# A list scheduler inside a two-block transformer kernel is run ten times, with backward priorities and margins in its cost table

## The chip, the cores and the metric

The kernel runs on one core of a Trainium2 chip. The metric is the device time of one execution in microseconds (us), less is better. Five engines run their own instruction streams and meet at semaphores: TensorE (PE in the rows, its weight loads PEld), VectorE (DVE), ScalarE (ACT), GpSimd (POOL) and SyncE (SP, which only issues transfers).

## What is computed

A sequence of 512 tokens of width 1024 passes two layers of a first block and one layer of a second block, all in fp32, and a final RMS norm. Cut to what matters:

```python
for l in range(2):                                   # first block
    sh1, sc1, gt1, sh2, sc2, gt2 = split(silu(c) @ w_ada[l] + b_ada[l])
    h = rms_norm(x) * (1 + sc1) + sh1
    dn_qkv, dn_z, dn_a, dn_b, sw_q, sw_k, sw_v, gate_a, gate_b = split(h @ w_in[l])
    o_dn = gated_delta_rule(l2(conv(dn_qkv)), g, beta)       # 8 heads of 128, state S
    y_a = (rms_norm(o_dn) * silu(dn_z)) @ w_dn_out[l]
    y_b = swa_sink_attention(sw_q, sw_k, sw_v) @ w_swa_out[l]   # window 128
    x = x + gt1 * ((sig(gate_a) * y_a + sig(gate_b) * y_b) @ w_o[l])
    h = rms_norm(x) * (1 + sc2) + sh2
    a, b = split(h @ w_up[l])                                # 2 x 2816
    x = x + gt2 * ((silu(conv(a)) * b) @ w_down[l])
# second block: band attention + S5 state space + GLU, gated merge, w_out, rms_norm
```

The delta rule is a recurrence over chunks: the state after one chunk is needed for the next (`v_new = u - w S; o = q S + qk v_new; S = S exp(g) + k^T v_new`), and inside a chunk a triangular system is solved.

## The kernel before, in words

**Matmuls.** Each fp32 operand is split in a high and a low part. A weight piece arrives by DMA as `raw` (128x1024), ACT rounds it to `whi`, and DVE takes `wlo = raw - whi`; activations give `hhi` and `hlo` in the same way. A product is then three matmuls, `hhi*whi`, `hlo*whi`, `hhi*wlo`, each with 512 columns, summed in PSUM in a tile `gf` (or `gt`, where the weights stand still). These are the bulk of TensorE's work, and they need nothing of the serial steps around them.

**The delta rule.** Two heads and four chunks at a time (a head pair) go through one chain, b = 0 to 3. On TensorE it reads: `yps` and `zps` in 32x32 tiles, twice, then `wps`, then `yps` and `zps` in 64x64 tiles (the inverse of the triangular system), then for each of four chunks `xps`, `osps`, `osps`, `kqs` (the recurrence). Each step's result is taken from PSUM by ACT (`y`, `yy`, `xs`, `qd`) or DVE (`xf`, `wf`, `st`, `pp`) before the next step can start. The products `qk` and the like of a chain are kept in four buffers of the tag `qk`; the evicted gate products `mb` use the buffers of that same tag.

**Attention and norms.** `sc` are scores, `pp` probabilities, `ptr` their transposes, `pc` and `pv` DVE's copies of them, `pvo` the product with the values. At the borders of the stages (mixing to FFN, FFN to mixing, FFN to the second block) the residual `x` is normed: `nsum` (the factor), `xn` (DVE), its transposes `ntr` (TensorE), again `xn` with scale and shift, then `hhi` (ACT) and `hlo` (DVE). Every weight product of the next stage needs these.

**The order.** Nothing of the order is written by hand. The program is recorded first: class `Recorder` keeps each engine call as an `Op` with its dependencies, the tiles it uses, and a duration from a table (`cost`). `plan` (line 202) is a greedy list schedule: at each step it takes the engine whose next ready op can start first, and on it the op of the least `prio`, which is the op's number in the program plus a bias that the network gives. A tile's buffers are given out in the order in which the program first uses the tiles of a tag. `emit` then issues all ops in the planned order (line 359, the line of every instruction in the profile) and fixes on each engine the order and who follows whom in each buffer. At run time each engine takes its instructions strictly in that order. So an instruction whose operand is late holds all that stands behind it on its engine.

## Time and profile before

| what | us |
|---|---|
| median of 3 runs | 2430.78 |
| lowest and highest | 2430.03, 2432.83 |
| profiled execution | 2433.17 |
| its span | 2431.4 |

The span reaches from the first to the last instruction of the profiled execution; 1.8 us lie around it. In the rows further down, a PE that is not busy is waiting, and the name behind the arrow is what released it. Matmuls overlap by their pipeline, so that the step from start to start, not the duration, is what one costs in a row of them. `f32` is named for both fp32 and the rounded form. In the rows of windows the granted clock (1.00 is TensorE's full 2.4 GHz, 0.50 the lower level of 1.2 GHz) is the third number from the end, behind the busy times of PE, PEld, DVE, ACT and POOL with their counts.

### The profile page before, as it was taken

To read this page: it belongs to the slowest core of one execution; us is meant where nothing else is said; L and a number is where in the kernel's file an instruction comes from. 1 tells how busy PE (TensorE), PEld (TensorE's weight loads), DVE (VectorE), ACT (ScalarE), POOL (GpSimd) and SP (SyncE) were. 2 spreads that over 40 slices of the span, in tenths; PEclk is the share of its full clock that TensorE was granted. 3 is DMA by queue.
4 is the path that set the end of the run, shared out by engine and by line. 5 is a ranking of instruction groups with operands and counts; after the bars stand their busy time and mean duration, and the time that the engine had idled before them with its cause. 6 is when DMAs were issued, how large, how long until landed. Compare 5 with 4: busy or idle time off the path is not lost.

```text
span 2431.4 us, 35819 instructions
## 1 busy us (share of the span) xinstructions
PE 2364.1 (97%) x13388; PEld 1928.4 (79%) x13388; DVE 1644.6 (68%) x3087; ACT 1012.2 (42%) x2095; POOL 522.9 (22%) x719
## 2 busy tenths in 40 slices
PE   7999999999999999999999999999999998999998
PEld 4878777778888887887888787888888888877786
DVE  3898899676666577468888955566555546765454
ACT  5544454533443233354446454334323323264432
POOL 1322424204100000213232421050051613500000
PEclk9999999999999999999999999999999999999999
DMA  7322225456446556332222333445334344532242
GB/s 251 99 66 77 84 71 161 139 168 200 156 153 197 180 181 187 118 103 74 66 75 79 89 111 96 130 170 184 114 109 127 117 146 146 173 113 79 78 139 78
DMA packets 239742, 309.10 MB, mean 127 GB/s; under 512 B 32144, under 2 KB 189712, under 8 KB 239568
## 3 DMA queue, kind: packets, MB, share of 16 engines
q1 hardware_dynamic: 228864, 275.64, 37.0%
q0 software_dynamic: 10416, 30.91, 3.5%
q8 instruction: 106, 1.74, 0.3%
q14 instruction: 68, 0.56, 0.1%
q10 hardware_dynamic: 288, 0.26, 0.0%
HBM read 276.20 MB, written 30.56 MB: 126 GB/s over the span
## 4 chain that ended last, share of the span: by engine, by line
PE 84%; DVE 7%; DMA 3%; ACT 2%; issue 2%; SPq 1%; POOL 1%; DVEq 0%; POOLq 0%; ACTq 0%
PE gf L359 54%; PE gt L359 18%; PE sc L359 1%; SPq L359 1%; PE pvo L359 1%; PE ada L359 1%; DMA pn<-nd 1%; PE zps L359 1%; PE osps L359 1%; PE kqs L359 1%; PE yps L359 1%; DVE wlo L359 1%; PE qktr L359 1%; PE gram L359 1%; DVE ua L359 1%
## 5 line engine op out<-in xcount | busy, mean ns | idle before, releaser
L359 PE MATMUL gf<-hhi,whi 128*128 128x512 f32 (+1 forms) x1888 | 720.8, 384 | 11.8 <-ACT whi L359 8.5
L359 PE MATMUL gf<-hlo,whi 128*128 128x512 f32 (+1 forms) x1888 | 720.6, 382 | 0.2 <-DVE hlo L359 0.2
L359 PE MATMUL gf<-hhi,wlo 128*128 128x512 f32 (+1 forms) x1888 | 719.9, 382 | 0.1
L359 DVE TENSOR_TENSOR wlo<-raw,whi 128x1024 fp32r<-128x1024 f32 (+1 forms) x358 | 461.8, 1291 | 339.2 <-ACT whi L359 336.1
L359 ACT ACTIVATE whi<-raw 128x1024 fp32r<-128x1024 f32 (+1 forms) x366 | 378.6, 1036 | 655.7 <-PE gf L359 310.5
L359 PEld LDWEIGHTS gf<-hhi,whi 128*128 128x128 f32 x1888 | 358.3, 191 | 76.2 <-ACT whi L359 10.0
L359 PEld LDWEIGHTS gf<-hlo,whi 128*128 128x128 f32 x1888 | 359.1, 190 | 60.7 <-issue 2.1
L359 PEld LDWEIGHTS gf<-hhi,wlo 128*128 128x128 f32 x1888 | 359.0, 190 | 59.4 <-DVE wlo L359 0.6
L359 PE MATMUL gt<-whi,g 128*128 128x512 f32 x704 | 220.1, 392 | 0.0
L359 PEld LDWEIGHTS gt<-whi,g 128*128 128x128 f32 x704 | 132.2, 188 | 27.2
L359 PE MATMUL gt<-wlo,g 128*128 128x512 f32 x352 | 137.4, 390 | 0.0
L359 DVE SCALAR_TENSOR_TENSOR acc<-raw,csil,acc 128x1024 f32<-128x1024 f32 x70 | 90.7, 1295 | 34.8 <-DMA raw<-in_w_ada_dram 34.6
L359 DVE SCALAR_TENSOR_TENSOR cacc<-gf,vec,cacc 128x511 f32<-128x511 f32 x144 | 106.8, 743 | 7.9 <-ACT cacc L359 6.6
L359 PE MATMUL gt<-whi,hhi 128*128 128x512 f32 (+1 forms) x288 | 107.1, 374 | 1.0 <-DVE gx L359 1.0
L359 PE MATMUL gt<-wlo,hhi 128*128 128x512 f32 (+1 forms) x288 | 107.6, 374 | 0.0
L359 PE MATMUL gt<-whi,hlo 128*128 128x512 f32 (+1 forms) x288 | 107.5, 375 | 0.0
L359 PE MATMUL gf<-rhi,whi 128*128 128x512 f32 x256 | 99.9, 390 | 0.0
L359 PE MATMUL gf<-rhi,wlo 128*128 128x512 f32 x256 | 99.8, 390 | 0.0
L359 PE MATMUL gf<-rlo,whi 128*128 128x512 f32 x256 | 99.8, 390 | 0.0
L359 DVE SCALAR_TENSOR_TENSOR facc<-gf,vec,facc 128x511 f32<-128x511 f32 x88 | 65.7, 748 | 37.2 <-ACT facc L359 35.6
L359 PEld LDWEIGHTS gt<-wlo,g 128*128 128x128 f32 x352 | 66.2, 188 | 13.5 <-issue 0.2
L359 POOL DMA_DIRECT2D acc<-in_b_ada_dram x4 | 2.1, 525 | 288.3 <-DVE wlo L359 283.5
(414 smaller groups left out, 3802.4 us busy)
## 6 DMA issues: line engine op xcount, KB each, us to landing
raw<-in_w_in_dram SPq DMA_DIRECT2D x140, 512.0 KB, 3.7
raw<-in_w_ada_dram SPq DMA_DIRECT2D x80, 512.0 KB, 4.0
raw<-in_w_up_dram SPq DMA_DIRECT2D x80, 512.0 KB, 4.2
raw<-in_w_down_dram SPq DMA_DIRECT2D x40, 512.0 KB, 3.7
wa<-in_w_ada_dram SPq DMA_DIRECT2D x32, 256.0 KB, 6.0
raw<-in_w_dn_out_dram SPq DMA_DIRECT2D x16, 512.0 KB, 3.5
raw<-in_w_swa_out_dram SPq DMA_DIRECT2D x16, 512.0 KB, 4.8
raw<-in_w_o_dram SPq DMA_DIRECT2D x16, 512.0 KB, 3.8
```

What stands on the lines that cost most here:

```text
L359: i = f(*a, **k).ins
```

## The change

The kernel's network, its instructions and its `cost` table stay. Only the planner is rewritten:

- `plan` is split. `prepare` builds what every schedule shares; `schedule(tags)` is the greedy pass, with buffers handed out in the order of `tags`; `late(seq)` walks a finished schedule backwards and gives each op the latest start that would not move its end, from the next op on its engine, its dependents, and the tile that follows in each of its buffers.
- `plan` now makes ten schedules. After each, the buffer order becomes the order of first use in that schedule, and the priority of each op becomes half its old priority (for the first, its start) plus half its latest start. The schedule with the least planned end goes out; here it is the third of the ten.
- `MARGIN`: 30 ns are added to each planned duration on every engine but TensorE. `SLACK`: 30 ns more on each crossing from one engine to another; it was zero.

```diff
-SLACK = {"PE": 0.0, "DVE": 0.0, "ACT": 0.0, "POOL": 0.0, "SP": 0.0}
+MARGIN, SLACK = 30.0, 30.0
+ROUNDS = 10
...
+    def schedule(self, tags):
...
+        place = {nm: (g, k) for g, names in tags.items() for k, nm in enumerate(names)}
...
-                since[tag, k] = t = heapq.heappop(freed[tag])
+                since[tag, k], old = heapq.heappop(freed[tag])
+                self.then[old] = tags[tag][k]
...
-                d = o.dur
+                d = o.dur + (0 if e == PE_E else MARGIN)
...
-                    q.ready = max(q.ready, clock[e] if q.eng == e == PE_E else end + LAT[q.eng] + (0 if q.eng == e else SLACK[q.eng]))
+                    q.ready = max(q.ready, clock[e] if q.eng == e == PE_E else end + LAT[q.eng] + (0 if q.eng == e else SLACK))
...
+    def late(self, seq):
+
+        late, after = {}, {}
+        for o in reversed(seq):
+            took, x = o.end - o.start, self.end
+            f = after.get(o.eng)
+            if f is not None:
+                x = late[f.n] - min(f.start - o.start, o.dur - o.over)
+            for q in o.succ:
+                if q.eng != o.eng or q.eng != PE_E:
+                    x = min(x, late[q.n] - took - LAT[q.eng])
+            for t in o.tiles:
+                if t.name in self.then:
+                    x = min(x, late[self.first[self.then[t.name]]] - took - 60)
+            late[o.n] = x
+            after[o.eng] = o
+        return late
+
+    def plan(self):
+
+        self.prepare()
+        tags, best = self.tags, None
+        for k in range(ROUNDS):
+            seq = self.schedule(tags)
+            if seq is None:
+                break
+            if best is None or self.end < best[0]:
+                best = self.end, seq
+            self.first, tags = {}, {}
+            for o in seq:
+                for t in o.tiles:
+                    if t.name not in self.first:
+                        self.first[t.name] = o.n
+                        tags.setdefault(t.tag, []).append(t.name)
+            late = self.late(seq)
+            for o in self.ops:
+                o.prio = 0.5 * ((o.prio if k else o.start) + late[o.n])
+        self.end, seq = best
         return seq
```

What this does to the streams is seen in the orders. Both programs hold the same matmuls; the FFN stages stand nearly as they stood, and most of what moved lies in the mixing stages of the first block and in the second block. The number of places where TensorE goes from one tile size to another falls from 213 to 186.

**First place: TensorE, last head pair (b = 3) of layer 0.** Before, the recurrence stands among the weight products `gf`. From the first chunk's `xps` (rows at TensorE's number 1344 and following):

```order
1344 L359 MATMUL xps<-vk,wf 128x128 x2
1345 L359 MATMUL gf<-hhi,wlo 128x512
1346 L359 MATMUL gf<-hhi,whi 128x512
1347 L359 MATMUL gf<-hlo,whi 128x512
1348 L359 MATMUL osps<-xs,kd 128x128 x2
1349 L359 MATMUL osps<-xs,ua 128x128 x2
1350 L359 MATMUL gf<-hhi,wlo 128x512
1351 L359 MATMUL gf<-hhi,whi 128x512
1352 L359 MATMUL gf<-hlo,whi 128x512
1353 L359 MATMUL gf<-hhi,wlo 128x512
1354 L359 MATMUL kqs<-st,qk 128x128 x4
```

Now the whole chain of this head pair stands bare, together with the last attention product in front of it; ahead of these rows stand four `ada` and eight `ptr`, and behind them three more rounds of `xps`, `osps`, `osps`, `kqs` follow before the next `gf` (number 1438):

```order
1417 L406 MATMUL pvo<-pc,swv 64x512 x2
1418 L406 MATMUL pvo<-pv,swv 64x512 x2
1419 L406 MATMUL yps<-xf,um 32x32 x32
1420 L406 MATMUL zps<-y_941,wf 32x32 x32
1421 L406 MATMUL yps<-xf,um 32x32 x16
1422 L406 MATMUL zps<-yy,wf 32x32 x16
1423 L406 MATMUL wps<-cst,xf 128x128 x8
1424 L406 MATMUL yps<-xf,ua 64x64 x8
1425 L406 MATMUL zps<-wf,yy 64x64 x8
1426 L406 MATMUL xps<-vk,wf 128x128 x2
1427 L406 MATMUL osps<-xs,kd 128x128 x2
1428 L406 MATMUL osps<-xs,ua 128x128 x2
```

What moved: the `gf` that stood between the steps have gone ahead of the chain or behind it. From the transposes to the last `kqs` no weight product is left to run while a step's result is being taken from PSUM.

**Second place: TensorE, the last rounds of the last head pair of layer 1.** Before, a few `gf` stand between every two steps:

```order
5192 L359 MATMUL xps<-pp,wf 128x128 x2
5193 L359 MATMUL gf<-hhi,whi 128x512
5194 L359 MATMUL gf<-hlo,whi 128x512
5195 L359 MATMUL gf<-hhi,wlo 128x512
5196 L359 MATMUL osps<-xs,kd 128x128 x2
5197 L359 MATMUL osps<-xs,ua 128x128 x2
5198 L359 MATMUL gf<-hhi,whi 128x512
5199 L359 MATMUL gf<-hlo,whi 128x512
5200 L359 MATMUL gf<-hhi,wlo 128x512
5201 L359 MATMUL kqs<-st,qk 128x128 x4
5202 L359 MATMUL gf<-hhi,whi 128x512
```

Now two rounds have none between them:

```order
5282 L406 MATMUL xps<-pp,wf 128x128 x2
5283 L406 MATMUL gf<-hlo,whi 128x512
5284 L406 MATMUL gf<-hhi,wlo 128x512
5285 L406 MATMUL osps<-xs,kd 128x128 x2
5286 L406 MATMUL osps<-xs,ua 128x128 x2
5287 L406 MATMUL kqs<-st,qk 128x128 x4
5288 L406 MATMUL xps<-pp,wf 128x128 x2
5289 L406 MATMUL osps<-xs,kd 128x128 x2
5290 L406 MATMUL osps<-xs,ua 128x128 x2
5291 L406 MATMUL kqs<-st,qk 128x128 x4
5292 L406 MATMUL gf<-hhi,whi 128x512
```

What moved: seven steps in a row stand without a `gf`.

**Third place: VectorE, the border from mixing to FFN in layer 0.** Here `xn` of the last tokens is what TensorE's `ntr` wait for. Before, two low parts `wlo` and both `hlo` stand between `nsum` and that `xn`:

```order
974 L359 TENSOR_TENSOR x<-x,xm 128x512
975 L359 TENSOR_SCALAR xn<-ntr,modc 128x128 x4
976 L359 TENSOR_TENSOR nsum<-nss 128x1
977 L359 TENSOR_TENSOR wlo<-raw,whi 128x1024 x2
978 L359 TENSOR_TENSOR hlo<-xn,hhi 128x4x128 x2
979 L359 TENSOR_SCALAR xn<-x,nsum 128x512 x2
980 L359 TENSOR_TENSOR wlo<-raw,whi 128x1024
981 L359 TENSOR_SCALAR xn<-ntr,modc 128x128 x4
```

Now:

```order
976 L406 TENSOR_TENSOR x<-x,xm 128x512
977 L406 TENSOR_SCALAR xn<-ntr,modc 128x128 x4
978 L406 TENSOR_SCALAR xn<-x,nsum 128x512
979 L406 TENSOR_TENSOR nsum<-nss 128x1
980 L406 TENSOR_TENSOR wlo<-raw,whi 128x1024
981 L406 TENSOR_TENSOR hlo<-xn,hhi 128x4x128
982 L406 TENSOR_SCALAR xn<-x,nsum 128x512 x2
983 L406 TENSOR_TENSOR hlo<-xn,hhi 128x4x128
984 L406 TENSOR_SCALAR xn<-ntr,modc 128x128 x4
```

What moved: one of the two `wlo` and one of the two `hlo` now stand behind that `xn`. On TensorE five rows of `gf` with 256 columns now stand ahead of the first `ntr` there, where `ntr` was the first.

## Rows read from the trace of the kernel before

**Rows 1.** page, engines: busy us (share of the span), instructions

```profile
...
PE 2364.1 (97%) x13388; PEld 1928.4 (79%) x13388; DVE 1644.6 (68%) x3087; ACT 1012.2 (42%) x2095; POOL 522.9 (22%) x719
...
```

**Rows 2.** stages: length, busy PE PEld DVE ACT POOL; granted clock, DMA share, GB/s

```profile
...
0.00:61.00 61.00, 46.95 (x241) 29.05 (x242) 19.60 (x44) 36.30 (x64) 12.09 (x18) 1.00 0.80 251
61.00:525.00 464.00, 453.29 (x3136) 362.51 (x3135) 395.63 (x955) 226.09 (x623) 136.44 (x139) 1.00 0.35 103
525.00:1060.00 535.00, 522.35 (x2499) 437.94 (x2498) 341.64 (x446) 187.39 (x271) 57.53 (x104) 0.98 0.54 170
1060.00:1504.00 444.00, 439.24 (x3102) 352.64 (x3101) 359.40 (x893) 219.48 (x610) 126.36 (x123) 1.00 0.30 85
1504.00:2060.00 556.00, 545.69 (x2655) 458.95 (x2654) 304.04 (x394) 193.29 (x279) 144.72 (x294) 0.98 0.42 137
2060.00:2420.00 360.00, 354.75 (x1759) 286.13 (x1758) 220.57 (x352) 148.93 (x250) 45.07 (x41) 1.00 0.35 112
...
```

**Rows 3.** what PE waited for: total us, times, longest

```profile
...
PE ntr L359 <- DVE xn L359: 11.2, 7, 4.0
...
PE gf L359 <- ACT whi L359: 8.5, 4, 3.2
...
```

**Rows 4.** same columns as Rows 2, around the dips of the clock

```profile
...
440.00:450.00 10.00, 7.76 (x27) 5.16 (x26) 9.32 (x28) 3.55 (x4) 0.52 (x1) 0.83 0.58 173
648.00:660.00 12.00, 7.61 (x42) 7.11 (x41) 10.53 (x20) 7.51 (x16) 2.04 (x2) 0.72 0.77 257
1028.00:1045.00 17.00, 10.90 (x57) 9.14 (x56) 14.05 (x29) 12.41 (x27) 3.91 (x4) 0.80 0.47 142
1644.00:1656.00 12.00, 8.41 (x52) 8.12 (x53) 9.69 (x19) 6.10 (x14) 2.04 (x2) 0.72 0.77 262
2019.00:2034.00 15.00, 9.79 (x46) 9.08 (x47) 11.07 (x24) 7.16 (x17) 4.48 (x3) 0.67 0.44 140
...
```

**Rows 5.** DVE and PE, first border between mixing and FFN: start, duration, idle before

```profile
650.63 2.35 DVE L359 TENSOR_TENSOR wlo<-raw,whi 128x1024 fp32r<-128x1024 f32 x2
...
654.64 1.75 PE L359 MATMUL ntr<-cst,xn 128*128 128x128 f32 x7 [1.16 <-DVE xn L359]
...
```

**Rows 6.** PE and DVE, last delta chain of layer 0: start, duration, operation

```profile
390.13 0.76 PE L359 MATMUL yps<-xf,um 128*32 128x32 f32 x64
...
402.86 3.00 DVE L359 TENSOR_TENSOR wlo<-raw,whi 128x1024 fp32r<-128x1024 f32 x1 [0.36 <-ACT whi L359]
...
403.51 1.14 PE L359 MATMUL zps<-wf,yy 64*64 64x64 f32 x16
...
407.21 0.60 PE L359 MATMUL xps<-vk,wf 128*128 128x128 f32 x4
...
411.80 0.68 PE L359 MATMUL xps<-pp,wf 128*128 128x128 f32 x4
...
417.30 0.39 PE L359 MATMUL xps<-pp,wf 128*128 128x128 f32 x2
...
420.83 1.13 PE L359 MATMUL kqs<-st,qk 128*128 128x128 f32 x8
...
```

**Rows 7.** that stretch in the columns of Rows 2, then gf alone

```profile
...
390.00:422.00 32.00, 32.00 (x370) 25.64 (x369) 29.53 (x69) 16.44 (x34) 14.07 (x24) 1.00 0.60 179
...
390.00:422.00 32.00, 21.99 (x76) 13.27 (x77) 1.27 (x2) 2.28 (x4) 1.00 0.60 179
...
```

**Rows 8.** PE, attention of layer 0, before and between two tiles

```profile
...
519.05 1.27 PE L359 MATMUL ptr<-cst,pp 128*128 128x128 f32 x8
...
522.77 1.08 PE L359 MATMUL pvo<-pc,swv 128*64 128x512 f32 x4
...
```

**Rows 9.** PE, around one piece of 128x32 tiles

```profile
...
394.42 0.39 PE L359 MATMUL gf<-hhi,whi 128*128 128x512 f32 x1
394.65 0.40 PE L359 MATMUL gf<-hlo,whi 128*128 128x512 f32 x1
394.98 0.70 PE L359 MATMUL yps<-xf,um 128*32 128x32 f32 x32
...
```

More of the change, by code (lines that the diff above doesn't have):

```diff
@@ L57 @@
 class Op:
-    __slots__ = ("n", "eng", "name", "call", "dur", "over", "lock", "dep", "succ", "left", "ready", "tiles", "need", "prio", "start", "mode", "bytes", "team", "lead", "wait", "tables")
+    __slots__ = ("n", "eng", "name", "call", "dur", "over", "lock", "dep", "succ", "left", "ready", "tiles", "need", "prio", "start", "end", "mode", "bytes", "team", "lead", "wait", "tables")
 class Eng:
@@ L199, in add, with prepare @@
         return o
-    def plan(self):
-        import heapq
+    def prepare(self):
         ops = self.ops
         for o in ops:
-            o.left = len(o.dep)
-            o.ready = 0.0
             for p in o.dep.values():
                 p.succ.append(o)
-        uses, order, bufs, place = {}, {}, {}, {}
+        self.uses, self.bufs, self.tags = {}, {}, {}
         for o in ops:
-            o.need = []
             for t in o.tiles:
                 nm = t.name
-                if nm not in uses:
-                    uses[nm] = 0
-                    tag = t.tag
-                    order.setdefault(tag, []).append(nm)
-                    bufs[tag] = t.bufs or t.tag_meta.bufs
-                    place[nm] = tag, len(order[tag]) - 1
-                uses[nm] += 1
-                o.need.append(place[nm])
+                if nm not in self.uses:
+                    self.uses[nm] = 0
+                    self.tags.setdefault(t.tag, []).append(nm)
+                    self.bufs[t.tag] = t.bufs or t.tag_meta.bufs
+                self.uses[nm] += 1
         pend = None
@@ L235, in plan @@
                 pend = (o, key) if o.mode != (128, 128) else None
+    def schedule(self, tags):
+        import heapq
+        ops, bufs = self.ops, self.bufs
+        uses = dict(self.uses)
+        place = {nm: (g, k) for g, names in tags.items() for k, nm in enumerate(names)}
         for o in ops:
-            o.left -= sum(p.lead is o.lead for p in o.dep.values())
+            o.need = [place[t.name] for t in o.tiles]
+            o.ready = 0.0
+            o.left = len(o.dep) - sum(p.lead is o.lead for p in o.dep.values())
             o.lead.wait = len(o.lead.team)
-        freed = {g: [0.0] * b for g, b in bufs.items()}
+        freed = {g: [(0.0, "")] * n for g, n in bufs.items()}
         turn = {g: 0 for g in bufs}
@@ L250, in plan @@
         count = 0
+        self.then = {}
         def offer(o):
@@ L262, in offer @@
                     return
-                since[tag, k] = t = heapq.heappop(freed[tag])
+                since[tag, k], old = heapq.heappop(freed[tag])
+                self.then[old] = tags[tag][k]
                 turn[tag] += 1
-                o.ready = max(o.ready, t)
+                o.ready = max(o.ready, since[tag, k])
                 o.need.pop()
@@ L286, in plan @@
         seq = []
-        import collections
         while count < len(ops):
@@ L300, in plan @@
             if best is None:
-                raise RuntimeError("no plan: slots %s" % {g: (turn[g], len(order[g]), sorted(parked.get(g, {}))[:3]) for g in turn if parked.get(g)})
+                return None
             s, e = best
@@ L314, in plan @@
                         heapq.heapify(av)
-                        heapq.heappush(av, (-1, x[1]))
+                        heapq.heappush(av, (-1e9, x[1]))
             p, n = heapq.heappop(av)
             for o in ops[n].team:
-                o.start = s = max(s, clock[e])
-                d = o.dur
+                s = max(s, clock[e])
+                d = o.dur + (0 if e == PE_E else MARGIN)
                 if e == PE_E and o.mode != mode:
@@ L328, in plan @@
                     held[e] = s + d
+                o.start = s
                 end = s + d
@@ L333, in plan @@
                     end = max(dma_free, end) + (2300 if e == SP_E else 2600)
+                o.end = end
                 count += 1
@@ L340, in plan @@
                     if not uses[nm]:
-                        heapq.heappush(freed[t.tag], last_end[nm])
+                        heapq.heappush(freed[t.tag], (last_end[nm], nm))
                         wake(t.tag)
@@ L350, in plan @@
         self.end = max(clock.values())
+        return seq
+    def late(self, seq):
[33 more added lines that the diff above has]
+        self.end, seq = best
         return seq
```

## The prediction, made before the changed kernel had run

> **What bounds the kernel now.** I read the engines first. TensorE is busy 97% of the span, VectorE 68%, everything else less [rows 1]. So the order can win only what TensorE waits, what it runs at the lower clock, and what it pays between tile sizes; all work of the other engines is hidden or lies inside these waits. The span of 2431.4 us less TensorE's busy 2364.1 leaves 67.3 us. That is the whole stock. The cut by stages says where it lies [rows 2]: 14.1 us in the first 61 us (61.00 less 46.95; the first weights are on their way), 10.7 in layer 0's mixing (61 to 525 us), 12.7 from there to 1060 us (layer 0's FFN with a border on each side), 4.8 in layer 1's mixing, 10.3 from 1504 to 2060 us (FFN and two borders), 5.3 in the second block, and 9.6 behind 2420 us, where the last norm is written.
>
> Second, the waits of TensorE by name. The largest off the start is `ntr` waiting for DVE's `xn`, 11.2 us in 7 times: the norm borders. Then `gf` waits for `whi`, 8.5 us in 4 times [rows 3]. Third, the clock. It stands at 1.00 in both mixing stages and dips at five places [rows 4]: around 445 us (0.83 over 10 us) and at the four borders (0.72 over 12 us, 0.80 over 17, 0.72 over 12, 0.67 over 15). What a dip costs is length times what is missing to 1.00: 1.7 us, and 3.4, 3.4, 3.4 and 5.0. The borders' own idle time is 4.4, 6.1, 3.6 and 5.2 us, together 19.3.
>
> **What the change removes.** The start and the end stand in the same order before and after, so 14.1 and 9.6 us stay. Of the rest I go by where the order moved.
>
> Layer 0's mixing has 10.7 us of scattered waits. In the new order nearly every chain but the last has more weight products between two steps than it had; I take 8 of the 10.7 as gone, and with them the dip at 445 us, 1.7 us, which began in two waits there (for `whi` and for the `wlo` behind it). Layer 1's mixing: 2 of 4.8. Second block: 1 of 5.3, since its order moved least where it waits.
>
> The borders: at the first one, DVE does two `wlo` (2.35 us) and two `hlo` between `nsum` and the last `xn`, and `ntr` waits at its end [rows 5]. With one `wlo` and one `hlo` behind `xn`, some 1.2 + 0.65 us of DVE's queue leave this path. But `hlo` is then late for the weight products behind, and the wait for `hhi` and `hlo` is next in line. I take 1 us for each border, 4 in all; nothing off the clock dips there, since the gap, if shorter, is still there.
>
> Tile sizes: a `gf` starts 0.23 us after the one before, but `yps` starts 0.33 us after its `gf` [rows 9], so a switch costs 0.1 us. The switches fall from 213 to 186: 27 x 0.1 = 2.7 us.
>
> Sum of gains: 8 + 1.7 + 2 + 1 + 4 + 2.7 = 19.4 us.
>
> **What the change adds.** The chain of layer 0's last head pair stands bare. Before, it ran from 390.13 us to 421.96 (420.83 + 1.13) [rows 6], 31.8 us, and TensorE had no idle moment in it: 32.00 of 32.00 busy [rows 7]. The weight products between the steps filled it: 76 `gf`, and at 0.23 us a step they were 17.5 us of work; counting what a stretched step gives, up to 19.9. So the chain's own matmuls are 12 to 14 us, and the rest was cover. In the new order there is no cover at all. TensorE takes its instructions in order, so each step waits for ACT or DVE to take the last one's result out of PSUM, and the `gf` that would fill the hole stand behind the chain. They are not lost, only displaced, and the stretch grows by the holes.
>
> How long is the chain alone? Not quite 31.8 us: some of its steps waited on DVE's other work. From `zps` at 403.51 to `xps` at 407.21 is 3.7 us, with a `wlo` of 3.00 in DVE's queue; alone I estimate 1.9. The three rounds from `xps` to `xps` or to the end took 4.59, 5.50 and 4.66 us; all at the shortest saves 0.9 more. That is 29.1 us alone, less 12 own, 17 us of holes. As bounds: with twice that trim 26.4 less 12, some 14; with no trim 31.8 less 12, some 20. Cover that could shorten it: DVE was busy 29.53 of 32 us there [rows 7], and some of that work still stands among the chain's steps, so I do not go under 14.
>
> In front of the chain the attention product is bare as well: `ptr` started at 519.05 and its `pvo` at 522.77 where other work stood between [rows 8], 3.7 us with DVE's copies `pc` and `pv` between; `ptr`'s own step is 1.0. So 2.7 us, from 0 (if the copies are quick) to 3.
>
> The clock in such a stretch: the trace has no stretch of 30 us with TensorE busy 40%. The nearest is the last border, 9.79 busy of 15 us, at 0.67, 5 us lost [rows 4]; around 445 us waits of about 3 us in sum were enough for 0.83. The floor is no loss, the ceiling that all 12 us of own work takes twice as long. I take the nearest row, 5 us, from 0 to 12.
>
> The Trainium skill ("TensorE: Matmul & The Clock Gate", section "Why this matters for your kernels") ties the drop of the clock to one long idle gap between bursts. By that rule the chain, whose holes are each about 1 us, would stay at 2.4 GHz and the 5 us would not arise; the rows around 445 us speak against it.
>
> In layer 1, two rounds of the last chain stand bare: four steps had three `gf` each (0.7 us) between them and have none. 4 x 0.7 is 2.7; I take 2.5, from 0 to 3.
>
> The margins cost nothing at run time: they are numbers of the planner. The transfers hardly moved on SP, and the weights' buffers hold some pieces ahead; I cost them at nothing. If that cover were gone, one late piece is a wait like those for `whi`, 8.5 us in 4 times [rows 3], about 2 us each.
>
> Sum of costs: 17 + 2.7 + 5 + 2.5 = 27.2 us.
>
> **Net.** 27.2 - 19.4 = +7.8 us. Against the profiled execution, 2433.2, that is 2441; against the median, which lies 2.4 us under it, 2430.8 + 7.8 = 2438.6 us.
>
> **Rivals.**
>
> A, faster: the bare chain is short and stays at full clock. Its place is rows 1416 to 1437 of TensorE's new order; its price is then 14 for the chain, 0 to 1 for attention, nothing for the clock, 1 in layer 1: 16 us. Against it stand gains of 19.4, and of up to 26 if the borders give 2 or 3 us each (19.3 idle and 15.2 of clock are there to be had). Time: 2430.8 + 16 - 25 = about 2422 us. For it: the waits that the new priorities go for are real and listed. Against it: DVE, the chain's partner, was 92% busy there. It decides when the stretch from `ptr` to the last `kqs` comes out under about 33 us at full clock (12 + 1 own, 19.4 gains).
>
> B, much slower: the clock goes to 1.2 GHz for most of the chain (+12 and not +5) and layer 0's waits only change place (gain 12 in all). 34.2 - 12 = +22: about 2453 us. For it: short waits pulled the clock down at 445 us. Against it: the other 7 us of waits in layer 0 left its clock at 1.00 over the stage [rows 2].
>
> C, no change: gains and costs meet, or the order does not matter since the same 67 us come back elsewhere: about 2431 us. Without the clock's 5 us and with 2 to 3 more of gains the sum lies here. The skill's rule on the clock, taken by itself, gives 2433.6, which lies here too.
>
> **Chances.** The forecast 0.50, with 2428 to 2448 as its own range; A 0.22; B 0.13; C 0.15. The measurement can tell about 0.2% from no change, 4.9 us: faster is under 2425.9, slower over 2435.6. Faster: A and little else, 0.24. Same: C and the low part of the forecast, 0.22. Slower: 0.54. The range takes in A's time and B's near part: 2420 to 2453 us.
>
> **What would show it.** In the new profile: a stretch of some 30 us in layer 0's mixing, near the end of the delta rule, where TensorE is busy about 40%, with `yps`, `zps`, `xps`, `osps` and `kqs` each waiting for `y`, `xf`, `xs`, `st` or `pp`, and the clock below 1.00 in it. The list of TensorE's waits should lose `gf` on `whi` around 440 us and name these steps instead, 17 to 20 us in sum. `ntr` on `xn` should fall from 11.2 to about 7 us. If the chain's stretch is much shorter than 26 us, or the clock holds, the forecast is too high; if the scattered waits of layer 0 are still there, it is too low.

## The result, and the profile after

The changed kernel takes 2457.55 us (median of 4 runs, 2454.9 to 2458.05) where the kernel before takes 2430.41 (4 runs, 2429.39 to 2432.83): ratio 1.0106, interval 1.0091 to 1.0121. That is 27 us slower between the medians (26 by the ratio), against 7.8 predicted, and 4.5 us above the upper end of the range. Slower was right; how much was not. The profiled execution took 2457.28 us with a span of 2455.5, 24.1 us over the span before, and the 24.1 are what the readings below account for.

The engines of after, from its page (busy us, share of the span, instructions):

```profile
PE 2374.6 (97%) x13388; PEld 1952.3 (80%) x13388; DVE 1641.4 (67%) x3087; ACT 1010.9 (41%) x2095; POOL 516.1 (21%) x719
```

TensorE is still 97% busy, and yet the span is longer by 1%: 13.7 us of the 24.1 are more idle time (a sum over its waits), and TensorE is busy 10.5 us more with the same 13388 matmuls [rows 1]. More busy time for the same work is the lower clock, whose mean over the span fell from 0.991 to 0.980, and so the page's first line hides nearly half of the loss.

The stages of after, in the columns of [rows 2] (length, busy of PE, PEld, DVE, ACT, POOL, clock, DMA share, GB/s):

```profile
61.00:525.00 464.00, 447.45 (x3048) 367.13 (x3046) 367.10 (x912) 218.15 (x597) 130.03 (x135) 0.96 0.34 99
525.00:1060.00 535.00, 523.88 (x2480) 435.30 (x2479) 350.56 (x477) 190.64 (x286) 61.79 (x108) 0.98 0.54 171
1060.00:1504.00 444.00, 435.53 (x3104) 362.02 (x3104) 344.35 (x841) 209.64 (x562) 122.61 (x115) 0.99 0.30 85
1504.00:2060.00 556.00, 537.17 (x2542) 443.23 (x2542) 325.87 (x445) 200.44 (x329) 139.92 (x295) 0.97 0.41 133
2060.00:2420.00 360.00, 356.63 (x1865) 293.35 (x1864) 216.89 (x343) 147.50 (x244) 46.43 (x41) 1.00 0.38 119
```

The windows are those of before, and the same work comes up to 25 us later in them. Layer 0's mixing has 16.6 us of idle time where it had 10.7, and 0.96 for its clock where it had 1.00. The stage from 1504 us on has 18.8 idle where it had 10.3; that one the prediction had not seen coming at all. The second block gained (3.4 for 5.3).

What TensorE waited for in after (total us, times, longest):

```profile
PE ntr L406 <- DVE xn L406: 10.0, 9, 2.1
PE gf L406 <- DVE wlo L406: 8.2, 7, 1.6
PE gt L406 <- DVE wlo L406: 6.6, 2, 6.1
PE sc L406 <- ACT pp L406: 5.0, 3, 2.6
...
PE xps L406 <- DVE pp L406: 3.5, 5, 1.3
PE kqs L406 <- DVE st L406: 3.0, 5, 1.3
...
PE gf L406 <- ACT whi L406: 0.8, 2, 0.4
```

`gf` on `whi` fell from 8.5 us to 0.8 [rows 3], as forecast. `ntr` on `xn` fell only from 11.2 to 10.0, and two new names stand beside it: `gf` and `gt` on `wlo`, 14.8 us together.

**Where the time went.** The two orders differ, so equal times of the two traces do not compare equal work. I gave every matmul its usual step, from start to start, in the trace of before (0.227 us for a `gf`) and read both traces at equal work done, some 2300 us in all. The difference between two such points is what a stretch cost. Other choices of the usual step move most rows by up to 3 us; the shape of the table stays:

| stretch (us of work) | predicted | measured |
|---|---|---|
| start and layer 0 up to its last head pair (0 to 320) | -9.7 | -10.4 |
| last head pair of layer 0 (320 to 440) | +24.7 | +24.9 |
| border, mixing to FFN | -1 | +2.5 |
| FFN of layer 0, its end (`sbt` on `modc`, 2.2 us before) | 0 | -2.9 |
| border, FFN to mixing | -1 | 0 |
| layer 1's mixing to 1280 | -2 | -8.5 |
| last head pair of layer 1 (1280 on) | +2.5 | +9.3 |
| behind it (`gt` on `mb`), and the third border | -1 | +4.9 |
| FFN of layer 1 (about 1840) | 0 | +8.2 |
| fourth border | -1 | +0.1 |
| second block | -1 | -3.5 |

The predicted 2.7 us for tile switches lie inside these stretches and cannot be told apart by it. The measured column sums to 24.6, against 24.1 of span; the rest is rounding and small steps.

**The bare chain of layer 0.** TensorE's timeline of after, with one row of ACT (start, duration, operation, idle before it and what ended it):

```profile
413.67 0.39 PE L406 MATMUL gf<-hhi,wlo 128*128 128x512 f32 x1
...
417.80 1.08 PE L406 MATMUL pvo<-pc,swv 128*64 128x512 f32 x4 [1.94 <-DVE pc L406]
...
421.53 0.96 PE L406 MATMUL zps<-y,wf 128*32 128x32 f32 x64 [1.10 <-DVE wf L406]
...
426.81 1.17 PE L406 MATMUL zps<-yy,wf 128*32 128x32 f32 x32 [1.20 <-ACT yy L406]
...
441.07 1.19 PE L406 MATMUL xps<-pp,wf 128*128 128x128 f32 x4 [0.53 <-DVE pp L406]
442.74 1.22 PE L406 MATMUL osps<-xs,kd 128*128 128x128 f32 x4 [0.47 <-ACT xs L406]
...
445.25 2.07 PE L406 MATMUL kqs<-st,qk 128*128 128x128 f32 x8 [0.44 <-DVE st L406]
...
453.77 1.09 ACT L406 ACTIVATE mb<-gf 128x512 f32<-128x512 f32 x2 [1.88 <-PE kqs L406]
454.43 0.79 PE L406 MATMUL gf<-hhi,whi 128*128 128x512 f32 x1 [0.26 <-ACT mb L406]
```

Between two weight products lie 40.8 us. Each step waits for its partner, as predicted, and no wait is longer than 1.94 us; 15 of them add up to 10.7. The durations tell the rest: eight matmuls of `kqs` take 2.07 us for the 1.13 of [rows 6], a `gf` 0.79 for the 0.39 of [rows 9]. The stretch and what follows it, in the columns of the stages:

```profile
413.60:454.50 40.90, 30.17 (x316) 24.02 (x314) 21.09 (x47) 12.33 (x26) 4.59 (x10) 0.63 0.27 79
454.50:460.00 5.50, 5.50 (x20) 4.72 (x21) 2.08 (x5) 3.33 (x11) 0.44 (x1) 0.63 0.03 10
```

The matmuls in it are worth 16.4 us at their usual steps (12.5 for the chain, 3.9 for `ada` and attention). So 24.3 us were lost: 10.7 waiting, and 13.7 in which TensorE is busy for longer than the usual steps. The clock, at 1.2 GHz from 424.4 to 458.5 us, is most of these 13.7 but not all. What it costs can be read from the run with the margins alone (below), where the same three rounds, from the first `xps` to the third `kqs`, stand without a weight product at full clock. That run first, then the change:

```profile
432.30:445.50 13.20, 9.38 (x60) 7.55 (x60) 4.19 (x16) 4.67 (x11) 0.44 (x1) 1.00 0.00 0
434.10:454.20 20.10, 16.29 (x62) 13.53 (x60) 4.21 (x15) 4.33 (x11) 0.58 (x1) 0.50 0.00 1
```

The idle time is 3.8 us at either level, and 6.9 us more of busy time are the clock's. Ahead of these rounds, from 424.4 us, TensorE is busy another 7.75 us at 1.2 GHz, of which at most half, 3.9, is the clock. So the clock cost at most 10.8 us here. The other 3 I take for the ends of short runs of matmuls, which have nothing behind them to overlap with; no run separates that.

**How many products there are to hide behind.** The `gf` at 413.67 is the 1248th weight product of the program and the one at 454.43 the 1249th. The 1248 fill the PSUM tiles of the gates; the next one has to wait for an eviction `mb`, and `mb` goes into a `qk` buffer, which the chain's last `kqs` sets free (the last two rows above say so). Before, 1105 products stood ahead of the chain's first step and 1180 were done at its last, so this limit was never met. After, all 1248 stood ahead, and the chain had none left. In layer 1 the counts ahead of the last chain are 4862 before and 5002 after, and the limit is at 5040.

**The long `wlo`.** In the FFN of layer 1 stands the largest new wait off the chains, where nothing of the order looked dangerous. VectorE and GpSimd, then TensorE, after:

```profile
1835.09 0.28 POOL L406 TENSOR_TENSOR sws<-pw,sbc 128x64 f32<-128x64 f32 x1
1835.28 11.95 DVE L406 TENSOR_TENSOR wlo<-raw,whi 128x1024 fp32r<-128x1024 f32 x1 [4.12 <-ACT whi L406]
1835.34 0.39 POOL L406 TENSOR_TENSOR stmp<-pw,sbm 128x128 f32<-128x128 f32 x1
...
1845.32 0.41 POOL L406 TENSOR_TENSOR sws<-sws,cst 128x128 f32<-128x128 f32 x1
...
1847.28 0.79 PE L406 MATMUL gt<-wlo,g 128*128 128x512 f32 x1 [6.11 <-DVE wlo L406]
```

Most `wlo` take 1.2 us; here one took 11.95, while GpSimd went through 37 small two-operand instructions without a pause. The clock stood at 0.83 over the 20 us around it.

### The profile page after: what moved, and what is told of

It is laid out like the page before. It is cut to its first block, busy times and chain, and to the rows that moved or that the text cites. A ratio compares the mean times of both kernels' runs of the same rounds, so it can differ in the third digit from the quotient of the medians.

```text
span 2455.5 us, 35847 instructions
## 1 busy us (share of the span) xinstructions
PE 2374.6 (97%) x13388; PEld 1952.3 (80%) x13388; DVE 1641.4 (67%) x3087; ACT 1010.9 (41%) x2095; POOL 516.1 (21%) x719
## 4 chain that ended last, share of the span: by engine, by line
PE 88%; DVE 5%; DMA 2%; ACT 2%; issue 2%; POOL 1%; SPq 1%; DVEq 0%; POOLq 0%; ACTq 0%
PE gf L406 56%; PE gt L406 19%; PE sc L406 1%; DVE wlo L406 1%; PE osps L406 1%; PE gram L406 1%; PE pvo L406 1%; PE kqs L406 1%; PE zps L406 1%; PE yps L406 1%; PE xps L406 1%; PE ada L406 1%; PE bs L406 1%; PE qktr L406 1%; DMA wa<-in_w_ada_dram 1%
## 5 line engine op out<-in xcount | busy, mean ns | idle before, releaser
L406 PEld LDWEIGHTS gf<-hhi,wlo 128*128 128x128 f32 x1888 | 360.7, 191 | 70.1 <-DVE wlo L406 10.5
L406 DVE SCALAR_TENSOR_TENSOR cacc<-gf,vec,cacc 128x511 f32<-128x511 f32 (+1 forms) x144 | 106.3, 742 | 9.7 <-ACT cacc L406 8.6
L406 PEld LDWEIGHTS gt<-wlo,g 128*128 128x128 f32 x352 | 66.6, 189 | 20.1 <-DVE wlo L406 6.5
L406 ACT ACTIVATE pp<-sc,snm 128x128 f32<-128x128 f32 x128 | 45.5, 365 | 46.1 <-DVE snm L406 36.4
```

What stands on the lines that cost most here:

```text
L406: i = f(*a, **k).ins
```

## The experiments

All kernels have the same network, and all but one the same instructions (one more has an added wait); what differs is the planner's constants, or the order after planning. Three questions: which part of the change costs, where, and by what mechanism. The edits are cut to what matters; names of orders and tiles are written out, and helper code is left out. Each ratio is to the kernel before, measured beside the run, with its 95% interval in brackets.

**Margins alone.** One schedule instead of ten.

```diff
-ROUNDS = 10
+ROUNDS = 1
```

> One schedule instead of ten, with the margins of 30 ns: program-order priorities and buffer order as before, only the planned durations and hops off TensorE are longer. Its order holds a stretch of 16 rows without a weight product at the last head pair of layer 0, behind the same 1248th weight product as in the changed kernel. Theory M (the margins bring the bare chain): at least 10 us over the kernel before, 2441 to 2452 us, and a stretch of 15 to 25 us in layer 0 with holes. Rival R (the backward priorities and the new buffer order bring it): within 4 us of before, 2427 to 2435.

2469.67 us, ratio 1.0152 [1.0137, 1.0167]: slower than the whole change, and by more than I had expected. Its two long waits at layer 0's end, and the two at layer 1's:

```profile
457.13 1.97 PE L406 MATMUL otr<-cst,ot 128*128 128x128 f32 x8 [8.45 <-POOL ot L406]
464.89 0.58 PE L406 MATMUL ada<-wlo,ones_r 128*1 128x512 f32 x1 [4.94 <-DVE wlo L406]
...
1470.84 1.97 PE L406 MATMUL otr<-cst,ot 128*128 128x128 f32 x8 [8.57 <-POOL ot L406]
1480.28 0.80 PE L406 MATMUL gf<-hhi,wlo 128*128 128x512 f32 x1 [5.96 <-DVE wlo L406]
```

Here the first half of layer 0's chain still has products between its steps, and only its rounds behind the 1248th product are bare; they run at full clock. But the chain ends late all the same, and what follows it (`ot`, its transposes `otr`) finds no product left to hide behind. Each layer's end costs 22.1 us against before. The margins by themselves bring the loss at the layers' ends.

**Backward priorities alone.**

```diff
-MARGIN, SLACK = 30.0, 30.0
+MARGIN, SLACK = 0.0, 0.0
```

> Ten schedules with backward priorities and buffer order, margins and slack zero. Theory M: no bare chain in layer 0, so the gains that showed elsewhere stay without that price, 2415 to 2430 us. Rival R: slower than before by 10 us or more, 2441 or higher.

2433.68 us (10 runs), ratio 1.0003 [0.9993, 1.0012]: no difference, and a time that neither theory gave. Theory M was right that the loss goes with the margins, and wrong that the gains stay. At equal work the kernel is 11.7 us ahead at 1070 us, and gives it back later. The largest piece goes in layer 1; VectorE, GpSimd and TensorE there:

```profile
1363.06 6.67 DVE L406 SCALAR_TENSOR_TENSOR rrs<-rnt,rrs 128x16 f32<-128x16 f32 x1
...
1363.61 2.41 POOL L406 TENSOR_TENSOR swq<-swq,rows 128x1024 f32<-128x1024 f32 x1
1365.97 2.51 POOL L406 TENSOR_TENSOR um<-ua,cst 128x512 f32<-128x512 f32 x2
...
1372.35 1.86 PE L406 MATMUL sc<-kT,qT 128*128 128x256 f32 x7 [4.80 <-ACT pp L406]
```

An instruction on 128x16 elements, 0.17 us elsewhere, took 6.67 while GpSimd ran back to back: it was locked out like the long `wlo`. A second one, a `wlo` of 6.80 us at 1586 us, costs 2.5 more.

**The order of before for layer 0, then that of the change.**

```diff
+PIECES = [("before", 1820), ("changed", INF)]   # up to which weight product
```

> The order of the kernel before up to the 1820th weight product (inside the FFN of layer 0), the order of the changed kernel behind it. If the stretches add up, the changed kernel's loss in layer 0's mixing (14.6 us net: 10 gained in its first part, 25 lost in its last) goes, and the time is 2457.5 - 14.6 = 2443 us, with the rest unchanged stage by stage. Rival: the stages are coupled (weights loaded ahead, buffers), and a good part comes back behind the cut, 2450 to 2457.

2442.32 us, ratio 1.0043 [1.0031, 1.0056], 15 us less than the change, as the table's first rows give (+14.5). The ten runs spread from 2435.87 to 2448.56, though, more than those of any other kernel here, and the profiled one took 2448.49: it has only 8.8 us less than the change. The long `wlo` of layer 1's FFN is there again, at 11.95 us. So the costs stay with their stretches, and the table may be read as a sum, to within some 6 us here; why this kernel spreads I did not find.

**GpSimd made to wait.** The next GpSimd instruction behind that `wlo` in the order gets a dependency on it.

```diff
+            if o.eng == DVE_E and o.tiles[-1].name == "wlo_3224":
+                gate = i.name
+            elif gate and o.eng == POOL_E:
+                self.tc.add_manual_dep(i, gate, sync, reason="port")
+                gate = None
```

> The changed kernel, with one wait added: in layer 1's FFN, GpSimd's next small operation waits until VectorE has done the one wlo that took 11.95 us there. Theory P (while GpSimd runs its small operations back to back, this wlo gets no turn): the wlo takes about 1.3 us, TensorE's wait of 6.1 us on it and the dip of the clock behind it go, 2457.5 - 8.2 = 2449 us. Rival: the wlo is slow for another reason (its operands, a transfer), it stays at about 12 us and the time at 2457.

2446.65 us, ratio 1.0057 [1.0042, 1.0072], 10.9 less than the change. The `wlo` before that one and the `wlo` itself, and GpSimd's wait for it:

```profile
1828.05 4.82 DVE L500 TENSOR_TENSOR wlo<-raw,whi 128x1024 fp32r<-128x1024 f32 x1 [2.71 <-ACT whi L500]
...
1833.49 1.23 DVE L500 TENSOR_TENSOR wlo<-raw,whi 128x1024 fp32r<-128x1024 f32 x1 [0.62 <-ACT whi L500]
1834.86 0.40 POOL L500 TENSOR_TENSOR stmp<-pw,sbm 128x128 f32<-128x128 f32 x1 [1.85 <-DVE wlo L500]
```

A pause of 1.85 us on GpSimd, and the `wlo` takes 1.23 us instead of 11.95. TensorE's wait of 6.11 is gone. The `wlo` ahead of it, which got no such pause, took 4.82. Three other kernels that leave this stretch as the change has it (layer 0 from before, the chain filled, the needless matmuls) have this `wlo` at 11.95, 12.12 and 11.38 us. This shows that GpSimd's uninterrupted stream makes VectorE's instruction long. Between the 6400th and the 6700th weight product, around it, the run gains 8.2 us on the change, which is what was expected; another 1.8 us it was ahead before that, where both programs have the same order, and these I can't put down to the wait.

**The chain filled again.** 48 products taken from ahead of the bare chain and put between its steps, the rest as in the change.

```diff
+FILLS = [("ptr_841", "kqs_977", [6, 0, 5, 6, 5, 4, 2, 2, 3, 2, 2, 2, 2, 2, 2, 2, 1])]
```

> The changed kernel, with the last 48 weight products that stand ahead of layer 0's last chain (10.9 us of work) moved in between its steps, 0 to 6 to a step; a few rounding steps of the weights follow later, all else stands as it was. Theory F (the products ran too early, and only lack in the chain): the chain is covered for 10.9 us and the clock holds, 2436 to 2445 us. Theory S (the serial chain, with the attention in front of it, comes too late, and the products that can run before its end are limited to 1248): the holes move into the attention ahead of the chain, the 1249th product starts as late as before, near 454 us, and the time is 2452 to 2460 us.

2458.38 us, ratio 1.0111 [1.0092, 1.0130]: as slow as the change. The waits, and the next product behind the chain:

```profile
406.04 2.07 PE L498 MATMUL sc<-kT,qT 128*128 128x256 f32 x8 [3.85 <-ACT pp L498]
413.33 1.94 PE L498 MATMUL ptr<-cst,pp 128*128 128x128 f32 x8 [3.51 <-DVE pp L498]
...
458.35 0.79 PE L498 MATMUL gf<-hhi,whi 128*128 128x512 f32 x1 [0.26 <-ACT mb L498]
```

The products now cover the chain, and their absence uncovers the attention ahead of it, which had leaned on them. The 1249th starts at 458.35 instead of 454.43, as theory S said. So the loss isn't that the chain is bare: the chain ends too late for the number of products that may run before its end, and the hole only moves.

**Margins of 20, one schedule.**

```diff
-MARGIN, SLACK = 30.0, 30.0
-ROUNDS = 10
+MARGIN, SLACK = 20.0, 20.0
+ROUNDS = 1
```

> One schedule with program priorities, margins of 20 ns in place of 30. Theory L (what counts is whether the last kqs of a layer comes before its 1248th weight product; the margin's size only shifts that by chance): its order has no bare stretch there, so it is within 10 us of the kernel before, 2423 to 2443. Theory M (margins cost by themselves, in proportion): two thirds of the 37 us that 30 ns cost, about 2457.

2455.01 us, ratio 1.0093 [1.0070, 1.0115]. Theory M's number; L's was missed. No bare run stands in its order, and still TensorE waits at the layers' ends, 3.61 us for `ot` and 5.82 for `wlo` at 443 to 450 us and 6.30 and 5.96 at 1451 to 1461.

**A mixture.** The order of the backward priorities without margins up to the 3620th weight product, that of before up to the 7700th, that of the change for the rest.

```diff
+PIECES = [("ten, no margin", 3620), ("before", 7700), ("changed", INF)]
```

> Ten schedules without margins up to the 3620th weight product (end of layer 0's FFN), the order of the kernel before from there to the 7700th, the changed kernel's order for the second block. If stretches add up: 2432.6 - 10.8 (layer 0 by the run with ten schedules alone) - 2.4 to 3.5 (second block) = 2418 to 2420 us. Rival (stages coupled): 2425 to 2433.

2422.33 us (2421.78 to 2423.7), ratio 0.9958 [0.9943, 0.9972]: faster than the kernel before and than the change, by 8.8 and 35 us. It is 2.3 us over the expected 2420, and under the rival's 2425. Its engines, from the page, and layer 0's stage, from the windows:

```profile
PE 2358.9 (97%) x13388; PEld 1925.7 (80%) x13388; DVE 1633.7 (67%) x3087; ACT 1011.5 (42%) x2095; POOL 518.8 (21%) x719
```

```profile
61.00:525.00 464.00, 458.43 (x3167) 366.95 (x3166) 391.11 (x959) 226.90 (x621) 135.87 (x140) 1.00 0.36 106
```

Layer 0's idle time is 5.6 us for 10.7 before. At equal work it is 8.6 us ahead at the end of that stage, 9.8 at the next border, and 10.6 ahead late in the second block: no locked-out instruction holds TensorE in the stretches taken from before. That is the gain that the change contained, without its margins.

**Margins of 35, ten schedules.**

```diff
-MARGIN, SLACK = 30.0, 30.0
+MARGIN, SLACK = 35.0, 35.0
```

> Ten schedules with margins of 35 ns. Its order has 21 rows without a weight product behind layer 0's 1248th, much like the changed kernel. Theory L: 15 us or more lost there, 2440 to 2465 us. Theory M (more margin, more loss): over 2460. If 35 ns come out near the kernel before (2427 to 2438), theory L is wrong on the price of a bare stretch.

2455.58 us, ratio 1.0087 [1.0067, 1.0106], inside L's range. Layer 0's end costs 14.6 us (up to 22 by other usual steps) and a `wlo` of 12.23 us at 1831 us another 9.3. So the time does not follow the margin's size from 30 to 35.

**Which margin: durations or crossings.** Two kernels, each with one schedule and 30 ns.

```diff
+MARGIN, SLACK, ROUNDS = 30.0, 0.0, 1
```

> One schedule, program priorities; 30 ns on each duration off TensorE, no slack on hops. By its order, 1190 weight products stand ahead of the first step of layer 0's last chain (before: 1105; changed kernel 1248), and 4974 ahead of layer 1's (4862; 5002). Theory D (the loss follows from how many products stand ahead of the last chain, since only 1248 and 5040 can run before its end): about 15 us lost at layer 0's end and 10 to 15 at layer 1's, 2448 to 2462 us. Rival H (the slack on hops, which stretches the chains themselves, does the harm): within 6 us of before, 2425 to 2437.

2467.32 us, ratio 1.0153 [1.0138, 1.0168]. That is 5 us over theory D's range, and far from H's. It has the same waits as margins alone (`otr` on `ot` 8.45 us at 449.47, then `ada` on `wlo` 4.94).

```diff
+MARGIN, SLACK, ROUNDS = 0.0, 30.0, 1
```

> One schedule, program priorities; 30 ns on each hop between engines, no margin on durations. 1133 products ahead of layer 0's last chain, 4858 ahead of layer 1's, near the kernel before (1105, 4862). Theory D: little lost at the ends of the layers (0 to 6 us), 2424 to 2437 us. Rival H: 2445 us or more.

2436.59 us, ratio 1.0027 [1.0016, 1.0038], inside D's range. The loss comes with the margins in the durations, nearly all of it; the crossings do little.

**The clock in the bare chain.** Needless matmuls, 2048 columns ahead of each step of layer 0's last chain, written to that step's own output tile before the step overwrites it: some 15 us of work that is of no use.

```diff
+for _ in range(2048 // n):
+    matmul(flat[:, 0:n], lhsT=h[:, 0, 0:128], rhs=h[:, 0, 0:n], start=True, stop=True)
```

> The changed kernel with needless matmuls (2048 columns, about 0.9 us, to a step) written into each step's own output tile ahead of the step itself, from layer 0's last attention product to its last kqs; they read resident activations and are overwritten. About 15 us of work is added into 41 us that held 13 us of useful work. Theory C (half of the price of this stretch is the clock, which stood at 1.2 GHz from 425 to 457 us): the clock holds at 2.4 GHz and the stretch from the 1248th to the 1249th weight product, 40.8 us, gets 3 to 8 us shorter in spite of the added work, 2450 to 2455 us. Rival W (the price is the waits of the serial chain alone, the clock only slows what would wait anyway): 2457 us or more, by what is added behind late operands.

2452.07 us, ratio 1.0095 [1.0078, 1.0112]: 5.4 us less than the change, with more work. The stretch:

```profile
413.90:451.50 37.60, 34.62 (x422) 29.34 (x421) 19.80 (x45) 11.04 (x24) 2.34 (x8) 1.00 0.23 70
```

TensorE is busy 92% there and the clock stays at 1.00. Yet from the 1248th product to the 1249th it is 40.3 us where it was 40.8. The needless work took the place of what the clock had cost, so the expected gain of 3 to 8 us is not in the stretch; the time fell into theory C's range for other reasons. In the stretch 0.5 us are gained, and behind it 1.9, since the first dozen products run at full clock. The rest of the lead can't be put down to the edit: 1.3 us of it are there before the first needless matmul, where both programs are the same (from 360 to 370 us TensorE is busy 7.86 us at a clock of 0.83 in the change, and 7.85 us at 1.00 here), and some 2.7 come up to the end of layer 1's mixing, in the same order as in the change.

**Negative margins, ten schedules.**

```diff
-MARGIN, SLACK = 30.0, 30.0
+MARGIN, SLACK = -20.0, -20.0
```

> Ten schedules, with 20 ns taken off each planned duration and each hop outside TensorE in place of 30 added. Its order lets 1064 weight products stand ahead of layer 0's last chain and 4858 ahead of layer 1's (before: 1105 and 4862; changed kernel: 1248 and 5002). Theory D (margins push the chains behind the products, the ends of the layers pay): the other sign of the margin costs nothing at the two ends, more short waits inside the layers, 2420 to 2437 us. Rival (any departure from the durations of the table costs, of either sign): 2445 us or more.

2462.35 us, ratio 1.0130 [1.0111, 1.0150]. Here my theory failed: I expected the chain early and the kernel near before. The chain is early (1064 products ahead of it, the fewest of all) and the layers' ends cost only 4.5 and 3.6 us. But TensorE waits in many places:

```profile
PE gf L406 <- DVE wlo L406: 8.8, 5, 2.3
PE ntr L406 <- DVE xn L406: 7.6, 6, 2.3
PE qktr L406 <- DVE qk L406: 5.1, 5, 1.9
PE otr L406 <- POOL ot L406: 4.7, 6, 1.4
```

There are 73 waits over 0.15 us for 43 before, 72.0 us of idle time for 57.7, and 27.2 us lost at the lower clock for 20.9. Of some 30 us, about 9 I could not place. So a plan that takes engines for quicker than they are came out as badly as one that takes them for slower. One rival stands untested: that any small change of the planned durations, of one or two nanoseconds, gives an order that is slower by chance. No run had so small a change.

**The counts together.** Weight products ahead of the first step of the last chain, and what the layer's end (320 to 440 us of work; 1280 to 1400) cost against before:

| kernel | layer 0: products | cost | layer 1: products | cost |
|---|---|---|---|---|
| margins -20, ten | 1064 | +4.5 | 4858 | +3.6 |
| before | 1105 | 0 | 4862 | 0 |
| no margins, ten | 1121 | -2.5 | 4910 | +6.1 |
| crossings only, one | 1133 | +8.1 | 4858 | -1.3 |
| 20, one | 1140 | +5.8 | 4954 | +14.4 |
| durations only, one | 1190 | +19.4 | 4974 | +15.9 |
| 30, one | 1224 | +22.1 | 4960 | +22.1 |
| 35, ten | 1243 | +14.6 | 4983 | +1.2 |
| the change (30, ten) | 1248 | +24.9 | 5002 | +8.3 |

A row can be off by 2 or 3 us, by the usual steps taken, and that of 35 ns in layer 0 by more. In layer 0 the five kernels under 1190 lose 8.1 us or less, the four from 1190 up lose 14.6 or more. Within the two groups, and in layer 1, the count does not sort them: there it matters as much what else stands at the end (`ot`, a locked-out instruction).

**Why longer planned durations put the chain late** I can argue from the orders, and did not show by a run. In the plan, a chain step waits for a VectorE or ACT operation that is 30 ns longer, and so is every operation queued before it; the greedy pass takes weight products for TensorE in the meantime. On the chip those engines are ready sooner, but TensorE keeps its order, products first. The head pairs slip one after the other: 408, 538, 689 and 1105 products ahead of the four chains before, 451, 614, 799 and 1248 after. That it is the margins that make them slip, the orders do show: 441, 604, 769 and 1224 with the margins alone, 423, 542, 699 and 1121 with the backward priorities alone.

## Why the prediction was wrong, point by point

**The bare chain: right in sum, wrong inside.** The steps "17 us of holes", "2.7" and "5 us" of clock gave 24.7; 24.3 were measured, and that is luck. The clock took up to 10.8 us, not 5, near the ceiling of 12; what is left for the serial chain and the attention is some 13.5, not 19.7. The chain from its first `yps` to its last `kqs` took 34.6 us, 24 of them without the clock's part, where "29.1 us alone" was estimated and 26.4 was the lower bound. Bare, the three rounds are at full clock (13.2 us) hardly shorter than three of the shortest before (4.59 each); it is the steps ahead of them that were put too long: 15.3 us of the 29.1, for 14.5 measured, some 10.6 without the clock's part. The rate of 5 us came from a border 15 us long [rows 4]; this stretch should have been costed at the lower level for most of its length, as rival B did, and rival B had this term nearly right. The Trainium skill ("TensorE: Matmul & The Clock Gate", section "Why this matters for your kernels") ties the drop to one long gap, which the longest gap here, 1.94 us, does not bear out. The Trainium skill ("TensorE: Matmul & The Clock Gate", section "A second HAM failure mode: psum-queue depth-cycling") tells, for another kernel, of many very short idle times that make the clock swing between its levels. The trace agrees that short idle times are enough; but here the clock did not swing, it stood at the lower level from 424.4 to 458.5 us.

**Layer 0's gains: right in number, partly by luck.** 9.7 predicted, 10.4 measured, and `gf` on `whi` all but gone. But the 1.7 us for the dip at 445 us, and the waits there, lie behind the stretch that gained 10.4. At about equal work, up to 361.1 us before and 349.4 after, TensorE's idle time fell by 6.5 us (21.35 to 14.81, 1 of them in the first 61 us, where nothing was forecast). Its busy time fell by another 5.2 (339.75 to 334.59), at a clock of 1.00 in both. This can't be waits; it is more than the 2.7 us that the forecast has for tile switches in the whole kernel. The new order goes from one kind of product to another less often there (241 times for 267 behind the first 70 us).

**Layer 1: both terms too small.** The gain was 8.5, not 2 (the idle time gives under 3 of it, the rest is again less busy time), and the cost 9.3, not 2.5. I costed four bare steps at 0.7 us. The two rounds' own waits are 3.2 us, but the attention ahead of them had lost its cover too. After, TensorE around 1388 us:

```profile
1384.58 0.74 PE L406 MATMUL sc<-kT,qT 128*128 128x256 f32 x4 [0.70 <-ACT osw L406]
1387.89 1.22 PE L406 MATMUL sc<-kT,qT 128*128 128x256 f32 x4 [2.57 <-ACT pp L406]
```

and the 15 us around, in the columns of the stages:

```profile
1380.00:1395.00 15.00, 11.73 (x46) 8.44 (x45) 12.62 (x23) 3.69 (x15) 6.51 (x8) 0.77 0.35 91
```

These 3.3 us of waits and 3.5 of clock (15 x 0.23) are the part that I had priced at nothing.

**The borders: wrong sign.** I took 1 us of gain at each; they cost 5.8 together (2.5, 0, some 3 of the third's 4.9, and 0.1). The step that failed is "`hlo` is then late for the weight products behind, and the wait for `hhi` and `hlo` is next in line": the name was wrong, it is `wlo`. First border, after:

```profile
665.97 0.66 PE L406 MATMUL ntr<-cst,xn 128*128 128x128 f32 x4 [1.32 <-DVE xn L406]
668.72 1.97 PE L406 MATMUL ntr<-cst,xn 128*128 128x128 f32 x8 [2.09 <-DVE xn L406]
672.43 0.58 PE L406 MATMUL gf<-hhi,wlo 128*128 128x256 f32 x1 [1.31 <-DVE wlo L406]
```

and the 16 us around, in the columns of the stages:

```profile
660.00:676.00 16.00, 10.43 (x50) 8.58 (x49) 12.81 (x24) 9.90 (x21) 4.10 (x3) 0.71 0.66 232
```

The `wlo` that was moved behind `xn` is waited for itself now, 1.31 us, and `ntr` still waits, in two pieces. TensorE idles 5.6 us in these 16 for 4.4 in the 12 of [rows 4], and what the clock lacks to 1.00 comes to 4.6 us (16 x 0.29) for 3.4: together about the 2.5.

**What was not seen: GpSimd.** "The margins cost nothing at run time" and "cost them at nothing" looked at SP and the transfers. That a shift of VectorE against GpSimd by a few microseconds could make one `wlo` ten times as long was in no term; it cost 8.2 us, by the table and by the run with the wait. The trace of before had the sign: a `wlo` of 3.00 us where others take 1.2 stood among my own rows [rows 6], and I put its length into the chain's price without asking what made it long. At the same place of the FFN, at 1815.84 us, two `wlo` took 5.99 us together in before, only that TensorE did not wait for them.

**In all.** Of what lies between forecast and result, on the scale of the span (24.1 less 7.8, which is 16.3), FFN 1 is 8.2 and the borders with the wait for `mb` 11.5 (7.5 for -4). Layer 1 nets 0.3 more than forecast; unforeseen gains at the FFN's end and in the second block, 5.4, go the other way. Layer 0 is 0.5 better than forecast, and the 2.7 for the switches, which the table counts within its stretches, come on top; that closes the 16.3 to within 1 us. So the steps that failed are the two terms that were taken as a gain or as nothing: the borders, and the margins' effect on VectorE beside GpSimd. The chain, on which nearly the whole prediction was spent, was wrong in its parts but is not the cause of the error in the sum.

## What to carry to other kernels

A margin in a static schedule for engines that keep their order is not slack: what waits in the plan is overtaken by filler, and on the chip it stays overtaken, so a serial chain can end late with nothing left to run beside it. Before a run, count how much filler may run before the chain's end (here 1248 products, by buffers) and how much of it stands ahead of the chain's start; if all of it does, the whole chain is paid for; here most of it ran at the lower clock too. When a reordering gains in one stage and loses in another, put the stages together from both orders: their costs added up to within a few us here, and the mixture gave 0.42%.

## What the runs showed of the hardware

**A VectorE instruction with two operands in SBUF can be kept out for many GpSimd instructions, not for one.** `wlo` took 11.95 us for 1.23 during 37 of them, and an instruction of 0.17 us took 6.67; with one pause of GpSimd, 1.23 again. The Trainium skill ("SBUF — State Buffer", section "Summary: rules for kernel authors") says that when a VectorE instruction with two SBUF inputs meets a GpSimd instruction that reads SBUF, the second to issue blocks until the first has finished. The runs agree that it blocks; that it got no turn between one GpSimd instruction and the next is more than the Trainium skill says there. It is not always so: the `wlo` of 3.00 us before [rows 6] got its turn behind one GpSimd instruction of 2.37 us, and GpSimd's next one then took 1.32 us for 0.46. What lets it in while GpSimd still runs, I could not tell.

**The clock goes to its lower level without a long idle time.** In the bare chain no gap was longer than 1.94 us. The clock fell to 1.2 GHz at 424.4 us, after waits of 1.94, 1.10 and 1.06 us, and stayed there until 458.5. The same bare rounds, with waits of 0.4 to 0.5 us, ran at 2.4 GHz throughout where they were entered at 2.4 (13.2 us, margins alone), and at 1.2 throughout where they were entered at 1.2 (20.1 us). With useless matmuls in the gaps the clock stayed at 2.4 GHz; that brought 2.4 us in the stretch and right behind it, for some 15 us of added work.
